# Order of two heads' products and Squares, of one subtraction, and the place of some weight tiles, in a hybrid decoder block

## The chip, the cores and the metric

The kernel runs on one core of one Trainium2 chip. The metric is the device time of one execution in microseconds (us), the median over several runs. A core has these engines: TensorE (PE in the profile; its weight loads, which overlap with its matmuls, are PEld), VectorE (DVE), ScalarE (ACT), GpSimd (POOL) and SyncE (SP), which here only issues transfers. Each engine has its own list of instructions and works through it in order; engines wait for each other on semaphores. SBUF is the on-chip memory that all engines read and write; PSUM is where TensorE puts its results, here cut into banks of 128 partitions x 512 fp32 numbers.

## The reference

One layer of a decoder block on x of 512 tokens by 1024 features, all in float32:

```
h   = rms_norm(x, norm_mix_pre)
proj = h @ w_in        # GLA q, k, v, r, a; NSA q and three branches' k, v; gates
A   = gla_mixer(...)   # chunked gated linear attention, 4 heads, dk 128, dv 256
B   = nsa_mixer(...)   # compressed, selected and window attention, 8 heads
mixed = sigmoid(merge_gla) * (A @ w_proj_gla) + sigmoid(merge_nsa) * (B @ w_proj_nsa)
x   = x + rms_norm(mixed @ w_out, norm_mix_post)
h   = rms_norm(x, norm_ffn_pre)
f   = (silu(h @ w_ffn_gate) * (h @ w_ffn_up)) @ w_ffn_down     # 1024 -> 2816 -> 1024
x   = x + rms_norm(f, norm_ffn_post)
```

The part of `gla_mixer` that the change touches, per head: the output of a chunk is the masked attention inside the chunk times v, plus q (with its decay) times the state before the chunk; then each token's 256 outputs are normalised by the root of their mean square and multiplied by a gate:

```
o = attn @ v + qe @ s_prev
o = o * rsqrt(mean(o * o) + eps) * norm_g
return o * silu(r)
```

## The kernel before, in words

**Three products for one.** A matrix in fp32 is split into a high part, rounded to the type fp32r, and a low part, the difference to it. `three` (L262 to L276) then makes one product out of three matmuls: high x high (L269), high weights x low data (L274), low weights x high data (L275). `prod` runs it over the 128-row blocks of the contraction. The product is [128 outputs, up to 512 tokens]; the activations h, transposed, lie in `hT` (`hT_hi`, `hT_lo`), the weights are the stationary operand. `split` (L299 to L303) makes the two parts: ScalarE writes the high one (L301), VectorE the low one (L303). For many weights `Stream.ahead_to` does the same at L103 and L110. A call of `restart()` makes the next product of 256 columns cut its second matmul into two of 128 columns.

**Fewer products.** Some large products are not done plainly but by a seven-product scheme for 2 x 2 blocks of matrices. Its units have seven products each, named `a11, s2, s3, s1, a22, s4, a12` after the weights' block or sum of blocks. In the first stage the units are those of the combined input projection (`EPAIRS`, functions `eproduct`, `eform`), in the last stage those of the down projection (`make`, `dsum`, `down_product`). Their matmuls have 256 columns, those of plain products 512.

**Weights in a ring.** `Ring` hands out the weight tiles: `whi0, wlo0, whi1, wlo1`, four tiles of 128 x 1024 fp32r that are used in turn. `Stream` loads a weight into a raw tile by a SyncE transfer, splits it into the next `whi` and `wlo`, and keeps one ahead of TensorE. Some keys have a place of their own (`place`) and take no ring tile. The ring is opened at the start (L181) and opened again at position 18 of the stream (`st.reset`, L119), at a new place of memory. Into the first ring go the weights of the token projection (keys `"tok"`), the forms of the seven-product units that `eplace` (L437) puts there two to a tile, and the plain products `with_gla`: GK0, GQ0, GK2, GQ2, MA0, MA1 (MA2 has a place of its own; MA3 lies in the second ring).

In the allocation of this kernel the first ring takes bytes 200,672 to 217,056 of a partition. Every tile in it starts at 224 modulo 256 bytes. `hT`, the moving operand of the plain products, starts at 160 modulo 256.

**The linear attention's stage**, about 60 to 227 us. `weave` lays the products of the seven-product units (main list) and the steps of the linear attention (side list) into one program order. `steps` has for head h: `gla_attn`, `gla_prep`, `gla_state`, `gla_out`, `gla_end`. `gla_out(h)` makes the head's output in four blocks n of 128 tokens, two blocks in each of two PSUM banks of the tag `acc`. For h of 0 and 1 a block is one or two plain fp32 matmuls (L806: attention x v; L808: q x state, from n = 1 on; each shows as two records in the trace), for h of 2 and 3 one or two calls of `three`. After each block ScalarE makes its Square with a sum over the 256 outputs (L809; it reads the bank and writes `go`):

```
out = ps[n // 2][:, (n % 2) * 256:(n % 2) * 256 + 256]
...
act.activation(out=o[:, n, :], in_=out, func=AF.Square, accum_out=ssq[:, n:n + 1])
```

The framework orders accesses by bank: an instruction that writes to a bank waits for an earlier one in program order that reads from it. Within the program order's dependences the framework may move instructions, so the trace has block 2 of head 1 ahead of block 1. Then follow the mean and root (`rsqrt_mean`, L317 on VectorE and L318 on GpSimd), the scaling of the four blocks (L817 on ScalarE), and in `gla_end` their transposes on TensorE (L832).

**The down projection's stage**, about 727 to 808 us. `seq` lists the seven-product units' products in order of use, number j; `make(j)` prepares the weights of product j some products ahead: `dsum` makes the sums and differences of raw blocks on VectorE, and `split` the two parts. Raw blocks are loaded on SyncE's queue as soon as a place is free (`dload`, L1899). The order on VectorE is the program order, except where `tc.issue_after(x)` puts an instruction behind x. The numbers that matter here: j = 7 is unit 1's `a11`, 8 `s2`, 9 `s3`, 10 `s1`, 11 `a22`, 12 `s4`, 13 `a12`. Unit 1's s4 is the block 12 of the raw weights less s2 (L1915), and the block 12 (`c_two`) is the last loaded. `lows[j]` is the low part's instruction of product j (L303).

Of the kernel before, what the change touches and what calls it, by code (L numbers as in the profile page):

```python
# [9 lines left out]
F32R = mybir.dt.float32r  # L10
U8 = mybir.dt.uint8
AF = mybir.ActivationFunctionType
OP = mybir.AluOpType
# [26 lines left out]
class Stream:  # L40
# [30 lines left out]
    def ahead_to(self, n, between=None):  # L71
        while self.made < min(n, self.limit or len(self.src)):
            i = self.made
            key, ap, cols = self.src[i]
            raw = self.raws.pop(i, None)
            if raw is None and key not in self.by_half:
                raw = self.fetch(i)
            if key in self.by_half:
                raw = self.pool.tile([128, 1024], F32, tag="wraw", bufs=3, name="wraw")
                hi = self.pool.tile([128, 1024], F32R, tag="whi", bufs=2, name="whi")  # L80
                lo = self.pool.tile([128, 1024], F32R, tag="wlo", bufs=2, name="wlo")
                big, small = ap
                b = big.shape[2]
                self.nc.scalar.dma_start(raw.rearrange("p (a t) -> p a t", a=2)[:, :, b:], small)
                for i2, c in enumerate((slice(0, cols // 2), slice(cols // 2, cols))):
                    self.nc.sync.dma_start(raw[:, c][:, :b], big[:, i2, :])
                    with self.tc.issue_after(last.ins) if i2 else nullcontext():
                        made = self.nc.vector.tensor_copy(hi[:, c], raw[:, c])
                    if i2 == 0:
                        last = between(made)  # L90
                    with self.tc.issue_after(last.ins):
                        self.nc.vector.tensor_tensor(out=lo[:, c], in0=raw[:, c], in1=hi[:, c].bitcast(F32),
                                                     op=OP.subtract)
                self.done[i] = (hi, lo)
                self.made += 1
                continue
            if key in self.place:
                hi, lo = self.place[key]()
            else:
                hi = self.pool.tile([128, 1024], F32R, tag="whi", bufs=2, name="whi")  # L100
                lo = self.pool.tile([128, 1024], F32R, tag="wlo", bufs=2, name="wlo")
            h, l, r = [self.part(key, x, cols) for x in (hi, lo, raw)]
            self.cast = self.nc.scalar.copy(h, r)  # L103
            if key in self.on_dma:

                self.nc.scalar.activation(out=l, in_=r, func=AF.Copy, scale=-1.0)  # L106
                self.nc.gpsimd.dma_start(l, r, accum_op=OP.add)  # L107
            else:
                with self.tc.issue_after(self.after.ins) if self.after else nullcontext():
                    self.nc.vector.tensor_tensor(out=l, in0=r, in1=h.bitcast(F32), op=OP.subtract)  # L110
                self.after = None
            self.done[i] = (hi, lo)
            self.made += 1
# [14 lines left out]
class Ring:  # L128
# [9 lines left out]
            self.pool[1].__exit__(None, None, None)  # L138
        self.pool = None

    def open(self, shift):

        self.close()
        p = self.tc.tile_pool(name="ring", bufs=1, reuse_waits="tile", side="right")
        self.pool = (p.__enter__(), p)
        self.turn = {"whi": 0, "wlo": 0}
        self.shift = shift

    def tile(self, shape, dtype, tag, bufs, name):
        if tag == "wraw":  # L150
            return self.raws.tile(shape, dtype, tag=tag, bufs=bufs, name=name)
        i = self.turn[tag]
        self.turn[tag] = i + 1
        t = self.pool[0].tile(shape, dtype, tag="%s%d" % (tag, i % 2), bufs=1, name=name)
        if self.shift and sum(self.turn.values()) == 4:
            self.pool[0].tile([128, self.shift], F32, name="shift")
        return t
# [17 lines left out]
def hybrid_block_kernel(ctx: ExitStack, tc: tile.TileContext, I, outT):  # L175
    nc = tc.nc
    act, dve, pool, pe = nc.scalar, nc.vector, nc.gpsimd, nc.tensor

    base = ctx.enter_context(tc.tile_pool(name="base", bufs=1, reuse_waits="tile"))
    wts = Ring(ctx, tc)  # L180
    wts.open(0)  # L181
    psum = ctx.enter_context(tc.tile_pool(name="psum", bufs=1, space=PSUM))

    def half_line(where):
# [55 lines left out]
    for key in with_gla + with_cmp + with_att + late:  # L240
        kind, n = key
# [343 lines left out]
    tok = [tokv.tile([128, 1024], F32, name="tok%d" % i) for i in range(NT)]  # L585
# [60 lines left out]
    lows = []  # L646
# [145 lines left out]
    def gla_out(h, after=None):  # L792
        q3, qk, ku, dec, kut, ss = gst[h]
        at = ats[h % 2]
        ps = [bank("acc"), bank("acc")]
        ssq = gt.tile([128, NT], F32, tag="gssq", bufs=2, name="gssq")
        o = gt.tile([128, NT, 256], F32, tag="go", bufs=1, name="go")
        for n in range(NT):
            out = ps[n // 2][:, (n % 2) * 256:(n % 2) * 256 + 256]
            if h >= 2:  # L800
                with tc.issue_after(after.ins) if after else nullcontext():
                    three(out, two_of[h, "a"][n], two_of[h, "v", n], True, n == 0)
                    if n > 0:
                        three(out, two_of[h, "q"][n], two_of[h, "s"][n - 1], False, True)
            else:
                pe.matmul(out, at[:, n, :], tok[n][:, h * 256:(h + 1) * 256], start=True, stop=(n == 0))  # L806
                if n > 0:
                    pe.matmul(out, q3[:, n].rearrange("p s t -> p (s t)"), ss[:, n - 1, :], start=False, stop=True)  # L808
            act.activation(out=o[:, n, :], in_=out, func=AF.Square, accum_out=ssq[:, n:n + 1])  # L809
        rs = gt.tile([128, NT], F32, tag="grs", bufs=2, name="grs")  # L810
        rsqrt_mean(rs, ssq, 256, EPS)

        def scaled(after=None):
            for n in range(NT):
                out = ps[n // 2][:, (n % 2) * 256:(n % 2) * 256 + 256]
                with tc.issue_after(after.ins) if after else nullcontext():
                    act.activation(out=o[:, n, :], in_=out, func=AF.Copy, scale=rs[:, n:n + 1])  # L817

        if h < 2:
            rest[h] = scaled  # L820
        else:
            scaled()
        gst[h] = o
# [1078 lines left out]
    def dsum(u, name, after=None):  # L1902
# [7 lines left out]
        elif name == "s1":  # L1910
            dve.tensor_tensor(out=r11, in0=r11, in1=draw[u, "s2"], op=OP.add)
            draw[u, "s1"] = r11
        elif name == "s4":
            x = draw[u, "s2"]
            dve.tensor_tensor(out=x, in0=r12, in1=x, op=OP.subtract)  # L1915
            draw[u, "s4"] = x


# [8 lines left out]
    def make(j):  # L1927
# [2 lines left out]
        u, a, b = seq[j]  # L1930
        behind = ends.get(j - 5) or ends.get(j - 7) if a == "s2" else None
        with tc.issue_after(behind.ins) if behind else nullcontext():
            dsum(u, a, (None, lows.get(7), None, ends.get(j - 3))[u])
        hi, lo = [x[:, :KW] for x in w_slot(("w", "g3", "w")[j % 3])]
        lows[j] = split(hi, lo, draw[u, a if a[0] == "s" else a[1:]])
        dw[u, a] = (hi, lo)
# [299 lines left out]
```

## Time and profile before

| | us |
|---|---|
| median of 3 runs | 829.97 (829.06 to 830.84) |
| profiled execution | 828.92 |
| its span | 826.7 |
| TensorE busy | 817.1 (99% of the span) |
| VectorE busy | 638.8 (77%) |
| ScalarE busy | 533.7 (65%) |
| GpSimd busy | 138.8 (17%) |

The profile is of one execution; the span goes from its first to its last recorded instruction, and 2.2 us of the execution's time lie outside it. A row of a timeline has the start in us from the span's start, the length in us, the engine, the line of the kernel, the operation, output and inputs by the program's names, the tile's shape, and the number of equal instructions that follow each other; in square brackets stands the idle time before it and what ended it. A matmul's length has its way through the array in it, and the next one starts before it ends: how long one takes in a stream is the distance from start to start. A row of a window has its limits, its length, the engine's busy time with the number of instructions, the granted clock of TensorE as a share of full speed, the busy share of the transfer engines and what they moved in GB/s.

### The profile page before, as it was taken

How to read it: one execution, taken by the hardware profiler on the slowest of the kernel's cores; microseconds unless marked ns; L12 is line 12 of the kernel's file. 1: busy time of each engine (PE TensorE's matmuls, PEld its weight loads, DVE VectorE, ACT ScalarE, POOL GpSimd, SP SyncE). 2: the span in 40 equal slices, each digit the busy share in tenths (PEclk: the TensorE clock that was granted, in tenths of full speed). 3: DMA queues.
4: the chain of work that ended last, by engine and by line, in shares of the span. 5: the costliest groups of instructions: out<-in, count | busy, mean ns of one | idle time of the engine just before them, and what ended most of it. 6: DMA issues, size and time to landing. Idle time of an engine off the chain costs nothing.

```text
span 826.7 us, 15082 instructions
## 1 busy us (share of the span) xinstructions
PE 817.1 (99%) x5751; PEld 751.2 (91%) x5751; DVE 638.8 (77%) x1216; ACT 533.7 (65%) x988; POOL 138.8 (17%) x172
## 2 busy tenths in 40 slices
PE   9999999999999999999999999999999999999997
PEld 7898899899888787888888999999999999999997
DVE  7776898886377888877666479998888778929886
ACT  6647677775544989887645577866665566626453
POOL 0101122230030000010000364111221110001134
PEclk9999999999999999999999999999999999999999
DMA  8434466764152444454227758798888883235233
GB/s 275 126 107 118 119 120 125 165 142 114 52 185 50 109 122 105 102 119 112 69 72 262 234 157 232 178 235 204 182 184 202 198 192 90 77 94 173 97 102 103
DMA packets 44824, 117.87 MB, mean 143 GB/s; under 512 B 5868, under 2 KB 12028, under 8 KB 44624
## 3 DMA queue, kind: packets, MB, share of 16 engines
q1 hardware_dynamic: 31584, 82.71, 32.5%
q0 software_dynamic: 12464, 33.85, 22.5%
q8 instruction: 45, 0.74, 0.4%
q10 hardware_dynamic: 704, 0.36, 0.1%
q14 instruction: 27, 0.22, 0.1%
HBM read 102.21 MB, written 4.19 MB: 129 GB/s over the span
## 4 chain that ended last, share of the span: by engine, by line
PE 89%; DVE 4%; ACT 4%; DMA 1%; issue 1%; POOL 0%; POOLq 0%; ACTq 0%; DVEq 0%
PE ps_mm L269 13%; PE ps_mm L274 13%; PE ps_mm L275 13%; PE ps_sc L269 5%; PE ps_sc L275 5%; PE ps_sc L274 4%; PE ps_acc L269 3%; PE ps_acc L274 3%; PE ps_acc L275 3%; PE ps_tp L275 3%; PE ps_tp L274 3%; PE ps_tp L269 3%; PE ps_sc L605 2%; PE ps_tp L605 2%; PE ps_tp L1246 2%; PE ps_mm L605 1%
## 5 line engine op out<-in xcount | busy, mean ns | idle before, releaser
L269 PE MATMUL ps_mm<-hT_hi,whi 128*128 128x512 f32 (+1 forms) x268 | 98.4, 367 | 0.0
L275 PE MATMUL ps_mm<-hT_hi,wlo 128*128 128x512 f32 (+1 forms) x268 | 96.9, 362 | 0.0
L274 PE MATMUL ps_mm<-hT_lo,whi 128*128 128x512 f32 (+1 forms) x267 | 96.3, 361 | 0.0
L103 ACT CAST whi<-wraw 128x1024 fp32r<-128x1024 f32 (+2 forms) x61 | 59.0, 970 | 51.2 <-PE ps_mm L274 15.3
L110 DVE TENSOR_TENSOR wlo<-wraw,whi 128x1024 fp32r<-128x1024 f32 (+2 forms) x46 | 50.1, 1091 | 29.9 <-ACT whi L103 29.8
L269 PEld LDWEIGHTS ps_mm<-hT_hi,whi 128*128 128x128 f32 x268 | 50.4, 188 | 8.1
L275 PEld LDWEIGHTS ps_mm<-hT_hi,wlo 128*128 128x128 f32 x268 | 50.4, 188 | 8.1 <-DVE wlo L110 0.3
L274 PEld LDWEIGHTS ps_mm<-hT_lo,whi 128*128 128x128 f32 x267 | 50.2, 188 | 6.6
L1576 ACT CAST d_two<-s 128x1024 fp32r<-128x1024 f32 x26 | 27.2, 1045 | 35.9 <-PE ps_mm L275 18.7
L303 DVE TENSOR_TENSOR pl<-ps_tp,ph 128x512 fp32r<-128x512 f32 (+1 forms) x64 | 31.2, 490 | 13.0 <-ACT ph L301 12.0
L1583 DVE TENSOR_TENSOR d_two<-s,d_two 128x1024 fp32r<-128x1024 f32 x25 | 30.6, 1225 | 11.3 <-ACT d_two L1576 10.9
L1208 ACT ACTIVATE p<-p,mx 128x512 f32<-128x512 f32 (+3 forms) x64 | 35.7, 558 | 4.6 <-DVE mx L1206 4.1
L1206 DVE CUSTOM_DVE_ANT_0 p<-ps_sc,causal 128x512 f32<-128x512 f32 (+3 forms) x64 | 30.1, 487 | 9.7 <-PE ps_sc L1200 8.9
L107 POOL DMA_DIRECT2D wlo<-wraw x15 | 12.7, 849 | 147.4 <-ACT wlo L106 90.2
L1981 POOL TENSOR_TENSOR y<-y,us 128x256 f32<-128x256 f32 x12 | 13.5, 1143 | 98.5 <-DVE us L1977 98.5
L301 ACT CAST ph<-ps_tp 128x512 fp32r<-128x512 f32 (+1 forms) x64 | 26.5, 416 | 4.4 <-PE ps_tp L1246 3.4
L1246 PE MATMUL ps_tp<-ident,p 128*128 128x128 f32 x160 | 27.7, 272 | 0.0
L1246 PEld LDWEIGHTS ps_tp<-ident,p 128*128 128x128 f32 x160 | 20.8, 141 | 7.2 <-ACT pc L1130 0.4
L1576 ACT CAST c_two<-s 128x1024 fp32r<-128x1024 f32 x12 | 12.5, 1044 | 20.3 <-PE ps_acc L275 10.5
L1558 POOL DMA_DIRECT2D wlo<-in_w_gate x13 | 11.2, 858 | 80.4 <-ACT wlo L1556 71.9
L269 PE MATMUL ps_mm<-hT_hi,d_two 128*128 128x256 f32 x80 | 22.4, 279 | 0.0
L275 PE MATMUL ps_mm<-hT_hi,d_two 128*128 128x256 f32 x80 | 22.3, 279 | 0.0
(905 smaller groups left out, 3299.5 us busy)
## 6 DMA issues: line engine op xcount, KB each, us to landing
wraw<-in_w_t SPq DMA_DIRECT2D x36, 512.0 KB, 4.0
wraw<-in_w_gate SPq DMA_DIRECT2D x21, 512.0 KB, 4.4
rw<-in_w_up SPq DMA_DIRECT2D x19, 512.0 KB, 8.2
wlo<-wraw POOLq DMA_DIRECT2D x15, 512.0 KB, 4.5
wlo<-in_w_gate POOLq DMA_DIRECT2D x13, 512.0 KB, 7.7
w_uu<-in_w_up POOLq DMA_DIRECT2D x19, 256.0 KB, 8.7
wraw<-in_w_proj SPq DMA_DIRECT2D x8, 512.0 KB, 3.5
wraw<-in_w_out SPq DMA_DIRECT2D x8, 512.0 KB, 4.3
```

What stands on the lines that cost most here:

```text
L103: self.cast = self.nc.scalar.copy(h, r)
L110: self.nc.vector.tensor_tensor(out=l, in0=r, in1=h.bitcast(F32), op=OP.subtract)
L269: pe.matmul(o, wh, xh, start=start, stop=False, skip_group_check=True)
L274: pe.matmul(o[:, c], wh, xl[:, c], start=False, stop=False, skip_group_check=True)
L275: stk["pe"] = pe.matmul(o, wl, xh, start=False, stop=stop, skip_group_check=True)
L303: return dve.tensor_tensor(out=lo, in0=src, in1=hi.bitcast(F32), op=OP.subtract)
L605: pe.matmul(o, x[:, k, t], y[:, w], start=(k == 0 and m == 0), stop=(k == KD - 1 and m == 2))
L1206: dve.tensor_tensor_reduce(out=o, in0=s, in1=causal[:, S - 128 * (i + 1):S], scale=-1.0, scalar=-NEG, op0=OP.add, op1=OP.min, accum_out=mx ...
L1208: act.activation(out=o, in_=o, func=AF.Exp, scale=-1.0, bias=mx[:, i:i + 1], accum_out=z[:, i:i + 1])
L1246: pe.transpose(tp[:, i * 128:(i + 1) * 128], p[:, OFF[i] + k * 128:OFF[i] + (k + 1) * 128] if i else p0, ident)
L1576: stk[names[0]] = act.copy(hi, t)
L1583: stk["lo"] = dve.tensor_tensor(out=lo, in0=t, in1=hi.bitcast(F32), op=OP.subtract)
```

## The change

Three edits that do not depend on each other.

1. In `gla_out` the Squares of blocks n - 1 and n are both issued in program order after the products of an odd n, where each had followed its own block's products.
2. In `dsum` the subtraction of unit 1's s4 is put behind `lows[j - 1]` on VectorE, the low part of product 11. The other units' s4 and the other sums stay as they were.
3. The first ring gets a little room: its `whi` tiles are 1072 wide and its `wlo` tiles 1040, and 1024 of that are used. A tile for a plain product (a key that is not `"tok"`) starts at element 48 of `whi` and at 0 of `wlo`; all others at 0 of `whi` and 16 of `wlo`. The ring's top stays, so that it begins 512 bytes lower, at byte 200,160 (224 modulo 256) of a partition. By these widths a plain tile comes to 160 modulo 256, and the others stay at 224. The second ring is opened without room, as before.

```diff
@@ Stream.ahead_to
-                hi = self.pool.tile([128, 1024], F32R, tag="whi", bufs=2, name="whi")
-                lo = self.pool.tile([128, 1024], F32R, tag="wlo", bufs=2, name="wlo")
+                plain = key[0] != "tok"
+                hi = self.pool.tile([128, 1024], F32R, tag="whi", bufs=2, name="whi", plain=plain)
+                lo = self.pool.tile([128, 1024], F32R, tag="wlo", bufs=2, name="wlo", plain=plain)
@@ Ring
-    def open(self, shift):
+    def open(self, shift, room=False):
         self.close()
+        self.room = room
...
-    def tile(self, shape, dtype, tag, bufs, name):
+    def tile(self, shape, dtype, tag, bufs, name, plain=False):
...
+        if self.room:
+            at = (0, 48) if tag == "whi" else (16, 0)
+            t = self.pool[0].tile([128, 1024 + max(at)], dtype, tag="%s%d" % (tag, i % 2), bufs=1, name=name)
+            return t[:, at[plain]:at[plain] + 1024]
@@ hybrid_block_kernel
-    wts.open(0)
+    wts.open(0, True)
@@ gla_out
-            act.activation(out=o[:, n, :], in_=out, func=AF.Square, accum_out=ssq[:, n:n + 1])
+            for m in range(n - 1, n + 1) if n % 2 else ():
+                act.activation(out=o[:, m, :], in_=ps[n // 2][:, (m % 2) * 256:(m % 2) * 256 + 256], func=AF.Square,
+                               accum_out=ssq[:, m:m + 1])
@@ dsum
         elif name == "s4":
             x = draw[u, "s2"]
-            dve.tensor_tensor(out=x, in0=r12, in1=x, op=OP.subtract)
+            with tc.issue_after(after.ins) if after and u == 1 else nullcontext():
+                dve.tensor_tensor(out=x, in0=r12, in1=x, op=OP.subtract)
@@ make
-            dsum(u, a, (None, lows.get(7), None, ends.get(j - 3))[u])
+            dsum(u, a, lows.get(j - 1) if a == "s4" else (None, lows.get(7), None, ends.get(j - 3))[u])
```

## The prediction, made before the result was known

> **What bounds the kernel now.** I read the page first.
>
> ```profile
> span 826.7 us, 15082 instructions
> PE 817.1 (99%) x5751; PEld 751.2 (91%) x5751; DVE 638.8 (77%) x1216; ACT 533.7 (65%) x988; POOL 138.8 (17%) x172
> ```
>
> TensorE is busy in 817.1 of 826.7 us; no other engine is above 77%. So an edit can win only where TensorE stands still, where it changes from one kind of matmul to another, or where one matmul takes longer than it need. The view of TensorE's waits, longest first, shows how little stands still:
>
> ```profile
> PE ps_acc L806 <- ACT go L809: 1.1, 1, 1.1
> PE ps_acc L215 <- DVE mhalf L200: 1.0, 1, 1.0
> ```
>
> So the third question matters most: how far apart do matmuls of one form start? The timeline of TensorE answers it for 512 columns, with first and last rows of two stretches of L269/L274/L275 alone (start, length, instruction):
>
> ```profile
> 89.75 0.40 PE L269 MATMUL ps_mm<-hT_hi,whi 128*128 128x512 f32 x1
> ...
> 97.92 0.39 PE L275 MATMUL ps_mm<-hT_hi,wlo 128*128 128x512 f32 x1
> ```
> ```profile
> 232.02 0.39 PE L269 MATMUL ps_mm<-hT_hi,whi 128*128 128x512 f32 x1
> ...
> 241.99 0.39 PE L275 MATMUL ps_mm<-gh,wlo 128*128 128x512 f32 x1
> ```
>
> 35 steps in 8.17 us are 233.4 ns each, 44 steps in 9.97 us are 226.6. For 256 columns I took windows with nothing else in them: length, busy time, matmuls (two of which were already running at the window's start), clock, DMA share, GB/s.
>
> ```profile
> 98.20:113.40 15.20, 15.20 (x131) 1.00 0.59 121
> 140.60:148.40 7.80, 7.80 (x71) 1.00 0.62 133
> 560.00:700.00 140.00, 140.00 (x1238) 1.00 0.78 181
> 771.00:808.00 37.00, 37.00 (x316) 1.00 0.31 101
> ```
>
> 15.20/129 = 117.8 ns, 7.80/69 = 113.0, 140.00/1236 = 113.3, 37.00/314 = 117.8. The clock is 1.00 in all and the slow stretches move the fewer bytes, so neither explains it. A 256-column stream has two paces and keeps one over a thousand matmuls.
>
> **The change, part by part.** The profiled execution took 828.92 us: the span of 826.7 and 2.2 outside it. It lies 1.05 below the median of 829.97. I sum against 828.92 and add 1.05 at the end.
>
> *Products ahead of Squares (`gla_out`).* No instruction is added or removed. Two n share a PSUM bank, so the product of n = 1 waited for the Square of n = 0 and that of n = 3 for the Square of n = 2. Head 1, TensorE and then ScalarE and VectorE:
>
> ```profile
> 160.76 1.02 PE L806 MATMUL ps_acc<-tok,at 128*128 128x256 f32 x4
> 161.62 0.59 PE L808 MATMUL ps_acc<-gs,gq 128*128 128x256 f32 x2
> 163.35 0.70 PE L806 MATMUL ps_acc<-tok,at 128*128 128x256 f32 x2 [1.14 <-ACT go L809]
> 163.89 0.59 PE L808 MATMUL ps_acc<-gs,gq 128*128 128x256 f32 x2
> ```
> ```profile
> 161.79 0.62 ACT L452 CAST whi<-wraw 128x512 fp32r<-128x512 f32 x1 [2.00 <-PE ps_acc L806]
> ...
> 162.84 0.36 ACT L809 ACTIVATE go<-ps_acc 128x256 f32<-128x256 f32 x1
> ```
> ```profile
> 161.80 0.69 DVE L388 TENSOR_TENSOR wraw<-wraw 128x512 f32<-128x512 f32 x1 [0.42 <-DMA wraw<-in_w_t]
> ```
>
> Four records of L806 take 161.62 - 160.76 = 0.86, so 0.215 each. The products of n = 0 and 2 run, then n = 1 waits for the first Square at 162.84, which is queued on ScalarE behind a cast whose data landed late (VectorE's row says so). The pair at 161.62 should end its issue at 162.05 and the next starts at 163.35: 1.30 lost; the two records after it take 0.54 for 0.43: 0.11. Head 1 is worth 1.41.
>
> Head 0 came in three visits; the last:
>
> ```profile
> 134.17 0.28 PE L269 MATMUL ps_mm<-et2gh,whi 128*128 128x256 f32 x1
> 134.52 0.70 PE L806 MATMUL ps_acc<-tok,at 128*128 128x256 f32 x2
> 135.06 0.59 PE L808 MATMUL ps_acc<-gs,gq 128*128 128x256 f32 x2
> ```
>
> 0.35 instead of 0.12 to enter and 0.54 instead of 0.43 behind it: 0.34. I take 0.3 for head 0; ends 0 (a wait for something else stands there) and 0.34. Heads 2 and 3 use three-part products. Their rows where a product follows a Square, first in head 2, then in head 3, and each head's transposes:
>
> ```profile
> 199.31 0.28 PE L274 MATMUL ps_acc<-gsgl,gqe 128*128 128x256 f32 x1
> 199.57 0.39 PE L269 MATMUL ps_acc<-tok,gah 128*128 128x256 f32 x1
> 199.79 0.28 PE L274 MATMUL ps_acc<-tok,gah 128*128 128x256 f32 x1
> ...
> 206.80 1.03 PE L832 MATMUL ps_tp<-ident,go 128*128 128x128 f32 x8
> ...
> 219.31 0.28 PE L274 MATMUL ps_acc<-gsgl,gqe 128*128 128x256 f32 x1
> 219.57 0.38 PE L269 MATMUL ps_acc<-tok,gah 128*128 128x256 f32 x1
> 219.80 0.28 PE L274 MATMUL ps_acc<-tok,gah 128*128 128x256 f32 x1
> ...
> 225.48 1.25 PE L832 MATMUL ps_tp<-ident,go 128*128 128x128 f32 x8
> ```
>
> 0.26 and 0.22 where 0.12 is the pace: 0.24 in each head. Head 3's transposes last 0.22 longer than head 2's, because the scaled blocks come late; products without a break bring the last Square forward, which should pay that. Head 2: 0.24, head 3: 0.45. Sum of this part: 1.41 + 0.3 + 0.24 + 0.45 = 2.4; ends 1.0 (head 1 alone, less 0.4 for a wait further on) and 2.44. What the edit delays is the Square of n = 0; behind it stand only the other Squares and the scaling, which needs all four anyway. No DMA is moved.
>
> *The sum behind a low part (`dsum`).* VectorE, TensorE and the chain of waits in the down stage:
>
> ```profile
> 766.81 1.09 DVE L1915 TENSOR_TENSOR c_two<-c_two 128x896 f32<-128x896 f32 x1 [1.01 <-DMA c_two<-in_w_down]
> 767.82 1.09 DVE L303 TENSOR_TENSOR wlo<-wraw,whi 128x896 fp32r<-128x896 f32 x1
> ...
> 770.15 1.08 DVE L303 TENSOR_TENSOR wlo<-wraw,whi 128x896 fp32r<-128x896 f32 x1
> ```
> ```profile
> 768.62 0.28 PE L274 MATMUL ps_tp<-dt3hl,whi 128*128 128x256 f32 x1
> 768.96 0.39 PE L275 MATMUL ps_tp<-dt3e,wlo 128*128 128x256 f32 x1
> 769.18 0.28 PE L269 MATMUL ps_tp<-dt3e,whi 128*128 128x256 f32 x1
> ...
> 776.25 0.28 PE L269 MATMUL ps_tp<-hT_hi,whi 128*128 128x256 f32 x1
> ```
> ```profile
> 760.82 5.89 DMA c_two<-in_w_down
> ```
>
> The subtraction of s4 waits on VectorE until its transfer has landed, 1.01 us idle, and the low part queued behind it (767.82) is the one that L275 needs at 768.96. That step is 0.34 for 0.113, the next 0.22: 0.33 lost. After the change this low part runs in the idle 1.01, and the subtraction stands behind the low part of 770.15, from about 771.3 to 772.4. Next late is its own cast (about 0.95 on ScalarE) and its low part (1.1): ready at 774.4. Its product starts at 776.25 and with what is won here before it (0.33, and 65 matmuls x 4.5 ns = 0.3) at 775.6: 1.2 us of cover, so I cost the move at nothing; without the cover it would cost what is late, up to 1.
>
> The stop at 768.62 is also where the pace goes from 113.3 to 117.8. If the stream is not interrupted, I expect it to keep 113.3: 314 matmuls of the last window, with those up to 771, about 335, x 4.5 ns = 1.5 us. Ends: 0 and 1.5. I take 1.5, as the 140 us of the third window kept it. Part: 1.85.
>
> *Weights 64 bytes lower (`Ring`).* In the kernel's allocation hT lies at 160 and every ring tile at 224, modulo 256 bytes of a partition. The wider tiles put the plain ones at 160. The stretch at 89.75 has weights 64 bytes off the moving operand, that at 232.02 has 0. Only GK and GQ twice and MA0, MA1 use this ring as plain tiles: 6 products x 24 = 144 matmuls x 6.8 ns = 0.98. Ends: 0 (place is not the cause) and 0.98; I take 0.7, nearer the upper end, as the first matmuls of each product may not be at their pace yet. The pair that follows at 98.2 inherits its pace from this stream: 129 x 4.5 = 0.6 if it falls to 113.3; even odds, so 0.3. The other entries into 256-column streams are drawn again, +-0.7. No instruction is added; the ring's larger reach only holds memory that nothing else uses at that time.
>
> The Trainium skill speaks against this part: "SBUF — State Buffer", Who interferes with whom, gives TensorE two independent read ports, one for the moving operand and one for weights, and lets TensorE wait on nobody. By that rule the places of two operands can't matter and this part is worth 0; the rows at 89.75 and 232.02 show two paces that the rule does not have.
>
> Sum: 2.4 + 1.85 + 0.7 + 0.3 = 5.25, less 0.5 because TensorE, coming earlier, meets transfers that did not move (161.80 is one). 4.75.
>
> **Rivals.**
>
> 1. *The pace does not hold in the down stage.* For: a pace is drawn at each interruption, and there are other ones near 768. Against: the third window. It costs 1.5: 826.7.
>
> 2. *Head 1's wait comes back.* The forms made at 161.79 are late because their data lands then; TensorE now arrives 1.4 earlier and waits for them in a later product. For: the row with 0.42 of waiting for that transfer. Against: no TensorE wait for such a form is among the longest. It costs 1.4: 826.6. With the first, 828.1.
>
> 3. *Place doesn't matter.* The last part gives neither 0.7 nor 0.3: 826.2. For: the two stretches above differ in more than the place. Against: nothing else in them differs by row or clock.
>
> 4. *Slower: a flip in the feed-forward stretch.* It holds 113.3 from one split matmul to the next:
>
> ```profile
> 555.01 0.33 PE L274 MATMUL ps_mm<-hT_lo,d_two 128*128 128x128 f32 x2
> ...
> 708.98 0.33 PE L274 MATMUL ps_sc<-hT_lo,whi 128*128 128x128 f32 x2
> ```
>
> One short stop of TensorE behind 555, because a ScalarE or transfer order has shifted, would leave the rest at 117.8: (708.98 - 555.01)/0.1133 = 1359 matmuls x 4.5 = 6.1 us: 831.3. It decides, that is eats the whole gain of 4.75, if it comes before 589 (4.75/4.5 ns = 1056 matmuls, 119.6 us before 708.98). For: 768.62 did just that. Against: nothing in the edits touches that stretch.
>
> **How the numbers follow.** 828.92 - 4.75 = 824.2 on the profiled basis, 825.2 on the median's. Chances: forecast 0.48, rival 1 0.16, rival 2 0.10, rival 3 0.08, two of these together or entries drawn badly (828 to 830) 0.09, rival 4 0.09. The range for 8 in 10 goes from 823.3 (1.9 less: 0.3 more from the places, 0.3 from the pair at 98.2, 0.5 without the loss to transfers, and 0.7 and a little for the entries) to 828.4 (rivals 1 and 2 together). About 0.2%, 1.66 us, is what a measurement of this kernel can tell from no change: faster means under 828.3, slower above 831.6. The first four cases are faster but for a remainder: 0.78. The fifth and half of the fourth rival: 0.14 the same. Half of rival 4 and mishaps with it: 0.08 slower.
>
> **What would show it.** Right: no wait of L806 for L809 around 161; L809 rows in twos behind n = 1 and n = 3; L303 at about 765.8 ahead of L1915; no step over 0.12 near 768.6 and over 325 matmuls in a window of the same 37 us there; 512-column steps of 227 before 98 and at 194 to 210. Wrong: a new wait of TensorE for a form between 165 and 180, a last window at 117.8, steps still at 233, or a count under 1230 in the 140 us behind 560.

## The result, and the profile after

The changed kernel takes 824.7 us (median of 6 runs, 823.91 to 826.72), the kernel before in the same comparison 829.43 (6 runs, 827.67 to 830.84). The ratio is 0.9947 with a 95% interval of 0.9930 to 0.9963: 4.4 us less, between 3.1 and 5.8 (the two medians themselves lie 4.7 apart). The forecast was 825.2 in a range of 823.3 to 828.4. The profiled execution has a span of 822.2 where the one before had 826.7.

In what follows line numbers of the changed kernel are higher than before: L813 and L815 are the plain products of `gla_out` (L806, L808), L276, L281 and L282 the three matmuls (L269, L274, L275), L310 the low part (L303), L1925 the subtraction of s4 (L1915), L841 the transposes (L832).

The page of the changed kernel, and the first and last of the four rows in its view of TensorE's waits:

```profile
span 822.2 us, 15085 instructions
PE 813.2 (99%) x5751; PEld 748.8 (91%) x5751; DVE 638.2 (78%) x1216; ACT 534.3 (65%) x988; POOL 138.5 (17%) x172
```
```profile
PE ps_acc L222 <- DVE mhalf L207: 1.1, 1, 1.1
...
PE ps_mm L612 <- DVE whi L88: 0.6, 1, 0.6
```

The wait of a product for a Square, first of the list before, is gone. The second row of the four is a wait of 0.7 for GpSimd at 28.8 us, far ahead of the change; the first profile of the kernel before does not have it, its second profile has it with 0.5. TensorE is as bound as it was, and busy for 4 us less. Its timeline at head 1, head 2, head 3's transposes, the second product at 92 us, product 9 of the down projection and that stage's end:

```profile
92.59 0.39 PE L282 MATMUL ps_mm<-hT_hi,wlo 128*128 128x512 f32 x1
...
98.03 0.39 PE L282 MATMUL ps_mm<-hT_hi,wlo 128*128 128x512 f32 x1
...
160.44 1.02 PE L813 MATMUL ps_acc<-tok,at 128*128 128x256 f32 x4
161.30 0.59 PE L815 MATMUL ps_acc<-gs,gq 128*128 128x256 f32 x2
161.74 0.59 PE L813 MATMUL ps_acc<-tok,at 128*128 128x256 f32 x2
162.17 0.59 PE L815 MATMUL ps_acc<-gs,gq 128*128 128x256 f32 x2
...
197.01 0.28 PE L276 MATMUL ps_acc<-tok,gah 128*128 128x256 f32 x1
197.13 0.28 PE L281 MATMUL ps_acc<-tok,gah 128*128 128x256 f32 x1
...
222.54 1.04 PE L841 MATMUL ps_tp<-ident,go 128*128 128x128 f32 x8
...
765.60 0.28 PE L281 MATMUL ps_tp<-dt3hl,whi 128*128 128x256 f32 x1
765.71 0.28 PE L282 MATMUL ps_tp<-dt3e,wlo 128*128 128x256 f32 x1
...
803.45 0.28 PE L282 MATMUL ps_sc<-hT_lo,wlo 128*128 128x256 f32 x1
803.83 0.61 PE L317 MATMUL ps_tp<-ones,acc 128*128 128x1 f32 x4
```

The plain products of head 1 follow each other without a break. The two steps of head 2 that were 0.26 and 0.22 are down to the pace, as the one from 197.01 to 197.13 shows, head 3's eight transposes last 1.04 and not 1.25, and there is no stop at product 9. From 92.59 to 98.03 are 24 steps, 226.7 ns each. The last two rows are new: 0.38 where 0.11 is the pace, a wait for the sums at the end of the stage.

VectorE in the down stage, and TensorE's window there, with the earlier line's columns:

```profile
764.22 1.09 DVE L310 TENSOR_TENSOR w_g3l<-wraw,w_g3h 128x896 fp32r<-128x896 f32 x1 [0.60 <-ACT w_g3h L308]
...
766.60 1.35 DVE L310 TENSOR_TENSOR wlo<-wraw,whi 128x896 fp32r<-128x896 f32 x1 [0.42 <-ACT whi L308]
767.87 1.08 DVE L1925 TENSOR_TENSOR c_two<-c_two 128x896 f32<-128x896 f32 x1
...
770.03 1.09 DVE L310 TENSOR_TENSOR wlo<-c_two,whi 128x896 fp32r<-128x896 f32 x1 [0.76 <-ACT whi L308]
```
```profile
767.00:803.00 36.00, 36.00 (x321) 1.00 0.30 96
```

The subtraction now comes behind product 11's low part, and no longer waits for its transfer. Product 12's low part is done at 771.1 and needed at 772.9, so the move costs nothing. 36.00/319 = 112.9 ns: the faster pace.

Where both traces pass the same matmul, and what each stretch contributed (starts in us, from the span's start):

| until | before | after | change in the stretch |
|---|---|---|---|
| first token sum in the attention stage | 65.22 | 65.73 | +0.51 (nothing of the change lies here; the wait at 28.8 us) |
| a product just ahead of head 0 | 127.42 | 127.54 | -0.39 (places 0.40, less a new stop of 0.24; the rest paces) |
| a product between heads 0 and 1 | 156.38 | 156.06 | -0.44 |
| product behind head 1 | 168.02 | 166.20 | -1.50 |
| MA0 | 194.29 | 192.55 | +0.08 |
| head 3's last transpose | 226.45 | 223.30 | -1.41 (heads 2 and 3 -1.2, places the rest) |
| product 9 of the down projection | 768.51 | 765.49 | +0.13 |
| product 12 | 776.25 | 772.62 | -0.61 |
| TensorE's last instruction | 820.92 | 816.45 | -0.84 |

The row of -0.39 can't be put down to the places as a whole: the same stretch took 61.64 to 62.21 in nine profiles of kernels that lack one edit or more, 61.77 in two that have none, as its 256-column streams ran at one pace or the other. What belongs to the places is read from their own products below.

### The profile page after: what moved, and what is told of

It reads as the page before. It is cut to its first block, busy times and chain, and to the rows that moved or that the text cites. A ratio compares the mean times of both kernels' runs of the same rounds, so it can differ in the third digit from the quotient of the medians.

```text
span 822.2 us, 15085 instructions
## 1 busy us (share of the span) xinstructions
PE 813.2 (99%) x5751; PEld 748.8 (91%) x5751; DVE 638.2 (78%) x1216; ACT 534.3 (65%) x988; POOL 138.5 (17%) x172
## 4 chain that ended last, share of the span: by engine, by line
PE 90%; DVE 3%; ACT 3%; issue 1%; DMA 1%; POOL 1%; SPq 0%; POOLq 0%; ACTq 0%; DVEq 0%
PE ps_mm L276 14%; PE ps_mm L281 14%; PE ps_mm L282 14%; PE ps_sc L276 4%; PE ps_sc L282 4%; PE ps_sc L281 4%; PE ps_acc L276 4%; PE ps_acc L282 4%; PE ps_acc L281 4%; PE ps_tp L282 3%; PE ps_tp L276 3%; PE ps_tp L281 3%; PE ps_tp L612 2%; PE ps_tp L1255 2%; PE ps_sc L612 1%; PE ps_acc L612 1%
## 5 line engine op out<-in xcount | busy, mean ns | idle before, releaser
L276 PE MATMUL ps_mm<-hT_hi,whi 128*128 128x512 f32 (+1 forms) x268 | 98.1, 366 | 0.0
L282 PE MATMUL ps_mm<-hT_hi,wlo 128*128 128x512 f32 (+1 forms) x268 | 96.6, 360 | 0.0
L281 PE MATMUL ps_mm<-hT_lo,whi 128*128 128x512 f32 (+1 forms) x267 | 96.0, 360 | 0.0
L276 PEld LDWEIGHTS ps_mm<-hT_hi,whi 128*128 128x128 f32 x268 | 50.4, 188 | 7.9
L282 PEld LDWEIGHTS ps_mm<-hT_hi,wlo 128*128 128x128 f32 x268 | 50.3, 188 | 7.9 <-DVE wlo L111 0.3
L281 PEld LDWEIGHTS ps_mm<-hT_lo,whi 128*128 128x128 f32 x267 | 50.2, 188 | 6.5
L310 DVE TENSOR_TENSOR pl<-ps_tp,ph 128x512 fp32r<-128x512 f32 (+1 forms) x64 | 31.2, 490 | 13.0 <-ACT ph L308 12.1
L108 POOL DMA_DIRECT2D wlo<-wraw x15 | 12.7, 849 | 147.4 <-ACT wlo L107 80.9
L276 PE MATMUL ps_mm<-hT_hi,d_two 128*128 128x256 f32 x80 | 22.3, 279 | 0.0
L282 PE MATMUL ps_mm<-hT_hi,d_two 128*128 128x256 f32 x80 | 22.3, 278 | 0.0
```

What stands on the lines that cost most here:

```text
L276: pe.matmul(o, wh, xh, start=start, stop=False, skip_group_check=True)
L281: pe.matmul(o[:, c], wh, xl[:, c], start=False, stop=False, skip_group_check=True)
L282: stk["pe"] = pe.matmul(o, wl, xh, start=False, stop=stop, skip_group_check=True)
L310: return dve.tensor_tensor(out=lo, in0=src, in1=hi.bitcast(F32), op=OP.subtract)
```

## The experiments

### One edit at a time

Three kernels, each the kernel before with one of the three edits as in the diff above.

> The kernel before with the order of products and Squares alone. My theory (a product of the second block of a bank waits for the Square of the first): the wait of head 1 is gone and stays gone, 2.4 us less than the kernel before, within 1.6 to 2.8; the stretch between the products of heads 0 and 3 carries it and nothing changes from 230 us on. Rival (the wait comes back where TensorE meets a form that was late anyway): at most 1.0 less, and a new row in the view of TensorE's waits.

Measured: 825.34 us beside 828.78 (12 and 35 runs), ratio 0.9964 (0.9952 to 0.9977): 3.0 us less, between 1.9 and 4.0, where 1.6 to 2.8 was expected. In the trace head 0's stretch falls from 9.00 to 8.58, head 2's from 9.72 to 9.25, head 3's from 9.35 to 8.67, head 1's from 8.78 to 7.28; no wait of a product for a Square and no new one behind. The mechanism is as expected; the size lies a little above the range. But this kernel, which has the old order in the down stage, showed neither the stop nor the slow pace there:

```profile
766.30 0.28 PE L274 MATMUL ps_tp<-dt3hl,whi 128*128 128x256 f32 x1
766.42 0.28 PE L275 MATMUL ps_tp<-dt3e,wlo 128*128 128x256 f32 x1
```
```profile
766.00:801.00 35.00, 35.00 (x312) 1.00 0.36 114
```

Product 9's third matmul starts 0.12 behind the second, and 35.00/310 = 112.9 ns.

> The kernel before with the subtraction of unit 1's s4 behind the low part alone. My theory: 0.33 us from the stop at 768.62 and 1.5 from the pace of 113.3 ns, which holds to the end of the stage: 1.85 less, within 1.4 to 2.0. Rival (the pace of this stretch comes from elsewhere): 0.33 less, and the windows behind 771 stay at 117.8 ns.

Measured: 827.84 beside 828.78, ratio 0.9996 (0.9984 to 1.0008): between 1.3 less and 0.7 more. That is not the 1.85 of the theory, and no clear gain at all. In its trace the stop is gone and the stage runs at 113.3 ns; but so did the kernel above without this edit.

> The kernel before with the places of the plain tiles alone. My theory (weights and moving operand at the same place modulo 256 bytes let a 512-column matmul start after 226.7 ns and not 233.4): 0.7 us less, within 0.2 to 1.3 with the 256-column stream behind it. Rival (the place does not matter): within 0.3 of the kernel before, and the two kinds of pace of 512-column streams mixed at random. The profile of the whole change speaks for something between: the first product still steps by 233, the others by 227.

Measured: 828.18 beside 828.78, ratio 0.9993 (0.9980 to 1.0006), which takes in both theories. The trace separates them: the 23 steps of the second product at 92 us are 226.7 ns each (233.4 before, 233.3 in the kernel with the sum alone). The two products up to 98 us take 0.31 less (10.96 for 11.27), GK0 and GQ0 with what lies between 0.20, the two stretches at 194 to 210 us 0.12 and 0.11: 0.74 in all. Something is given back: behind the first product of the pair at 98 us TensorE now waits, by the profile for a copy of ScalarE, and two steps there are 0.27 and 0.22 long, some 0.25 lost. The first twelve steps of the pair take 1.56 for 1.41; in the five profiles with these places and no added cuts they take 1.52 to 1.57, in the eight without these places 1.36 to 1.41. In its down stage TensorE stopped longer than before and kept the fast pace all the same:

```profile
767.39 0.28 PE L281 MATMUL ps_tp<-dt3hl,whi 128*128 128x256 f32 x1
768.08 0.38 PE L282 MATMUL ps_tp<-dt3e,wlo 128*128 128x256 f32 x1 [0.41 <-DVE wlo L310]
```
```profile
770.00:803.00 33.00, 33.00 (x294) 1.00 0.36 115
```

A stop of 0.58 (0.69 less the step), then 33.00/292 = 113.0 ns. A stop is not enough to set the slow pace.

### Is the place the cause, and the pace a state?

```diff
@@ Ring.tile, the kernel with the places alone
-            at = (0, 48) if tag == "whi" else (16, 0)
+            at = (0, 16) if tag == "whi" else (48, 0)
```

> As the kernel with the places alone, but with the plain tiles at 32 modulo 256 bytes, 128 bytes away from the moving operand (element 16 of whi and 0 of wlo; the others at 0 and 48). My theory (only the same place modulo 256 brings 226.7 ns): the two products at 87 to 98 us step by 230 or more, and nothing is gained beside the kernel before. Rival (any place but 64 bytes away, or chance): steps of 227 there and 0.3 to 0.7 less.

Measured: 828.26 beside 828.30, ratio 0.9997 (0.9980 to 1.0014). The 23 steps at 92 us are 232.1 ns each, and the two products up to 98 us take 11.22 (11.27 before, 10.96 with the places of the change). So room in the ring does nothing; of the three distances tried, 64, 128 and 0, only 0 is fast. The time alone could not have told it. The moving operand stayed where it was in all of these kernels, so they do not separate the distance from the weights' place itself. This run also has a small hitch at 754.77, far ahead of product 9, and behind it the slow pace:

```profile
754.77 0.32 PE L276 MATMUL ps_mm<-hT_hi,w_g3h 128*128 128x256 f32 x1
754.92 0.28 PE L281 MATMUL ps_mm<-hT_hi,w_g3h 128*128 128x256 f32 x1
```
```profile
757.50:803.00 45.50, 45.50 (x389) 1.00 0.40 135
709.00:754.00 45.00, 45.00 (x400) 1.00 0.29 80
```

A step of 0.15 for 0.11 was enough: 45.50/387 = 117.6 ns behind it, 45.00/398 = 113.1 ahead.

```diff
@@ hybrid_block_kernel, the kernel before
     for j, (u, a, b) in enumerate(seq):
+        if j == 10:
+            restart()
         end = down_product(j)
```

> The kernel before with no edit of the change, but with the second matmul of product 10 of the down projection cut in two of 128 columns, as at the other restarts. It leaves the stop at 768.62 in place. My theory (a pace is a state, set at an interruption and kept until the next; a cut matmul sets the faster one): the stop still costs 0.33, the windows from 772 on are at 113.3 ns, and the time is 1.4 us less. Rival (the 117.8 comes from what the other engines and transfers do there, or from the late sums): nothing gained, the windows stay at 117.8.

Measured: 828.4 beside 828.78, ratio 1.0000 (0.9987 to 1.0014): no gain of 1.4. The trace shows the mechanism as expected, though:

```profile
768.61 0.39 PE L275 MATMUL ps_tp<-dt3e,wlo 128*128 128x256 f32 x1
768.84 0.28 PE L269 MATMUL ps_tp<-dt3e,whi 128*128 128x256 f32 x1
...
770.95 0.28 PE L269 MATMUL ps_tp<-dt1e,w_g3h 128*128 128x256 f32 x1
771.07 0.33 PE L274 MATMUL ps_tp<-d_two,w_g3h 128*128 128x128 f32 x2
```
```profile
772.00:803.00 31.00, 31.00 (x276) 1.00 0.33 108
```

Behind the stop 18 steps take 2.11 us, 117 ns each; behind the cut matmul 31.00/274 = 113.1. So the pace is a state that an interruption can change either way, and a cut can set it back. That it was worth nothing in the median fits with the other profiles of kernels without the edit of the sum, of which only two in seven are in the slow pace there.

```diff
@@ the changed kernel
     def eproduct(u, i):
+        restart()
...
     def ffn_half(e, w, ps, ks=range(KD)):
+        restart()
...
     def out_half(n, e):
+        restart()
```

> The changed kernel, with the second matmul cut in two at the start of every product of the first seven-product units and of every call of the half-width products between 455 and 520 us. Theory (each interruption draws the pace again, a cut matmul sets the faster one and costs nothing): the 256-column steps at 117.8 between 80 and 200 us and between 470 and 520 us fall to 113.3, by the steps in the changed kernel's trace 2.2 us in all; 1.2 to 2.4 less than the changed kernel. Rival (the cut matmul costs something each time, or the pace is set by the weights' and data's places): no gain on the changed kernel, or slower.

Measured: 837.38 beside 828.30 for the kernel before, ratio 1.0105 (1.0085 to 1.0126): 8.7 us slower than before and some 12.7 slower than the changed kernel. A cut is not free, as I had assumed:

```profile
107.03 0.28 PE L276 MATMUL ps_mm<-hT_hi,feq 128*128 128x256 f32 x1
107.15 0.33 PE L281 MATMUL ps_mm<-hT_lo,feq 128*128 128x128 f32 x2
...
107.49 0.28 PE L276 MATMUL ps_mm<-hT_hi,feq 128*128 128x256 f32 x1
```

Three matmuls take 0.46 where three uncut ones take 0.34. The page counts 5,843 matmuls for 5,751, so 92 more: 92 x 0.113 = 10.4 us, most of the loss. Some of the rest are waits of 0.2 to 0.6 us that the changed kernel does not have. Nor does a cut always set the faster pace: behind 9 of the 63 cuts between 77 and 201 us the steps stayed at 117.5 ns or more. Where it does, it pays by these numbers from some 25 matmuls of the slow pace on (0.113/0.0045).

### How much is drawn anew in each execution?

> The kernel before once more, unchanged, for its profile alone: which of its stops are drawn anew in each execution? If head 1's wait hangs on when a transfer lands, the stretch of 159 to 168 us lies anywhere from 7.3 to 8.8 us; if the 117.8 ns of the down stage is a drawn state, it may be 113.3 this time. If both are fixed in the kernel, they come back as 8.78 us and 117.8 ns.

Measured: one run of 826.88 us, span 824.7, and a profile without any of the stops on which much of my sum rested. Head 1 of this second profile of the kernel before, and its down stage:

```profile
161.36 1.02 PE L806 MATMUL ps_acc<-tok,at 128*128 128x256 f32 x4
162.22 0.59 PE L808 MATMUL ps_acc<-gs,gq 128*128 128x256 f32 x2
162.66 0.59 PE L806 MATMUL ps_acc<-tok,at 128*128 128x256 f32 x2
```
```profile
160.83 0.62 ACT L452 CAST whi<-wraw 128x512 fp32r<-128x512 f32 x1 [0.40 <-DMA wraw<-in_w_t]
...
161.99 0.39 ACT L809 ACTIVATE go<-ps_acc 128x256 f32<-128x256 f32 x1
```
```profile
770.00:803.00 33.00, 33.00 (x294) 1.00 0.33 104
```

ScalarE's cast, held by the transfer, began 0.53 ahead of the first product; in the first profile it began 1.03 behind it (161.79 and 160.76). The Square then comes in time, and n = 1 follows without a wait. The transfer behind that cast took 4.64 us from issue to landing here and 6.27 in the first profile. Count the cast's start from the product 1.5 us ahead of the head, in all kernels without added copies: with the old order, starts of 0.79 to 1.12 go with stretches of 7.26 to 7.35, and starts of 1.92 to 2.61 with 8.05 to 8.78. With the new order a start of 1.83 still goes with 7.28. The down stage runs at 33.00/292 = 113.0 ns.

> The changed kernel once more, for its profile alone. Theory: 7.28 us in head 1's stretch again, because nothing is left to wait for; 0.43 less in head 0 (8.57 between its two marks), 0.45 to 0.7 less in heads 2 and 3; the down stage at 113.3 ns unless something else stops TensorE there.

Measured: 824.78 us, span 822.6; head 1's stretch 7.35, head 0's 8.56, head 2's and 3's as in the changed kernel, down stage at the fast pace. As expected.

### Making ScalarE late on purpose

```diff
@@ gla_out, in both kernels, ahead of the loop over n
+        for _ in range(3 if h == 1 else 0):
+            act.copy(o[:, 2:4, :].rearrange("p a b -> p (a b)"), at.rearrange("p n t -> p (n t)"))
```

> The kernel before with three extra copies of 128x512 on ScalarE (some 0.52 us each by the rows of its casts) ahead of the first Square of head 1, which writes over what they leave. Theory (before the change, TensorE's second block of a bank waits for the first block's Square, so that all lateness of ScalarE in head 1 reaches TensorE): a wait of L806 for L809 of 1 to 2.7 us in head 1, in whatever state the transfer lands, and 0.8 to 1.6 more than the kernel before. Rival (the wait of 1.14 in the first profile was a matter of the late transfer alone, and ScalarE has slack for the copies): no wait above 0.6, same time.

> The changed kernel with the same three copies at the same place. Theory (after the change no product of head 1 waits for a Square): no wait of a product in head 1, the stretch from 159 to 168 us as in the changed kernel (7.28 us between the products named et3gh and hT there) to 0.3, and at most 0.3 more than the changed kernel in time. Rival (lateness only moves to the forms behind the Squares on ScalarE): a new wait of TensorE of 0.5 us or more between 163 and 180 us.

Measured: the kernel before with the copies 828.11 beside 829.14 (ratio 0.9989, 0.9970 to 1.0008), the changed one with them 825.36 (0.9956, 0.9937 to 0.9976). The copies did not do what they were for: ScalarE took them at 150 to 155 us, in idle time. The profile of the first is of use for another reason, since in it the transfer landed latest of all, 7.05 us behind its issue:

```profile
163.30 0.62 ACT L452 CAST whi<-wraw 128x512 fp32r<-128x512 f32 x1 [2.81 <-DMA wraw<-in_w_t]
...
164.35 0.36 ACT L811 ACTIVATE go<-ps_acc 128x256 f32<-128x256 f32 x1
```
```profile
161.41 1.02 PE L808 MATMUL ps_acc<-tok,at 128*128 128x256 f32 x4
162.27 0.59 PE L810 MATMUL ps_acc<-gs,gq 128*128 128x256 f32 x2
164.86 0.82 PE L808 MATMUL ps_acc<-tok,at 128*128 128x256 f32 x2 [2.00 <-ACT go L811]
165.47 1.06 PE L810 MATMUL ps_acc<-gs,gq 128*128 128x256 f32 x2
```

The cast is 1.51 later than in the first profile (163.30 and 161.79), and so is the product that resumes (164.86 and 163.35). Head 1's stretch is 11.19. In the changed kernel with the copies it is 7.34, with a transfer of 4.90.

```diff
@@ gla_out, the kernel before (the changed kernel: (h, n) == (1, 1))
+            for _ in range(5 if (h, n) == (1, 0) else 0):
+                act.copy(o[:, 3, :], out)
             act.activation(out=o[:, n, :], in_=out, func=AF.Square, accum_out=ssq[:, n:n + 1])
```

> The kernel before with five copies of 128x256 on ScalarE out of the bank of head 1's first product, ahead of its Square; since they read that product they cannot run early, as the three copies of the late kernels did (ScalarE took them in idle time at 150 to 155 us). By the step from one Square to the next half of a bank (0.26 to 0.28 us) they hold ScalarE 1.3 to 1.4 us. Theory (a bank's second product waits for all that reads its first): TensorE waits in head 1 in every execution, the stretch between the marks et3gh and hT is 8.4 us or more (7.3 without a wait), and the time at least 0.8 more than the kernel before. Rival (slack on ScalarE takes it): stretch under 8, same time.

> The changed kernel with the same five copies, out of head 1's first bank, behind its two products and ahead of their Squares. Theory: no product of head 1 waits; the stretch between the marks stays at 7.3 us and the time within 0.4 of the changed kernel. Rival (ScalarE, 1.3 us later, holds up a form that TensorE needs next): a stop of 0.3 us or more between 163 and 180 us and 0.5 to 1.3 more.

Measured: 828.87 beside 829.79 (ratio 0.9993, 0.9981 to 1.0006) and 825.7 (0.9948, 0.9929 to 0.9966). The theory for the first failed: its stretch is 7.63, not 8.4, and the time is not longer. The framework had put the held products elsewhere:

```profile
162.39 0.48 PE L269 MATMUL ps_mm<-et1gh,whi 128*128 128x256 f32 x1
...
163.52 0.70 PE L806 MATMUL ps_acc<-tok,at 128*128 128x256 f32 x2
...
165.07 0.59 PE L806 MATMUL ps_acc<-tok,at 128*128 128x256 f32 x2
```

Lateness that is written into the program was filled here with matmuls of another product; the waits that these profiles show came with a transfer, whose lateness the program does not hold. In the second kernel the copies did hold the Squares: counted from the same product ahead of the head, the first began after 4.86 us, where it was 2.99 in the second profile of the changed kernel. Head 1's stretch was 7.35 all the same, as expected, and no stop above 0.2 followed up to 180 us. So with the new order Squares that are 1.9 us late cost nothing here. Its profile is also the only one of a kernel with all three edits that fell into the slow pace: from 758 to 804 us 391 matmuls, 117.6 ns each, behind steps of 0.23 at 750.50 and 0.16 at 755.27. So the edit of the sum does not guard the pace.

## Why the prediction was right, point by point

The number was right, 825.2 for 824.7, and so was the sign of each edit's cause in the attention stage. But two terms stood for events of one execution, and one of them did not belong to the edit.

*Head 1, 1.41.* The mechanism is right, the size is that of one draw. Six profiles of kernels with the old order and no copies in this stage gave 8.78, 8.74, 8.05, 7.35, 7.28 and 7.26 for the stretch, by when the transfer landed; five with the new order gave 7.28 to 7.35. On the mean over these the edit is worth 0.6 here, and 1.1 with the profile of 11.19, whose copies ran in idle time and whose transfer was merely the latest. It takes a risk away rather than a cost.

*Heads 0, 2 and 3, 0.3 + 0.24 + 0.45.* Undersized: 0.43, 0.47 and 0.68, and these came back in every profile. In head 0 two visits to the plain products replace three, and none waits. In heads 2 and 3 the step and the one behind it are gone from both places where a product had followed a Square, of which I priced one. With head 1's 0.6 to 1.1 this part is 2.2 to 2.7, for 2.4 forecast; the time of this edit alone says 1.9 to 4.0.

*Squares' lateness at nothing.* Held: no form behind them became late, and the rival with a new wait (2) did not happen in any profile.

*The sum, 1.85.* Here a step failed: "If the stream is not interrupted, I expect it to keep 113.3." It does; but I took the slow pace of one profile for what the kernel does. Of seven profiles of kernels without this edit, and without a cut there, two had the slow pace (the first profile, and the places at 128, from 754 us on), and of five with it one had it. The stop itself, with the slower step behind it, was worth anything from 0 to 0.72; it is what the edit seems to take away, since none of the five kernels with it stopped at product 9 and four of the seven without it did, one by 0.03 only. The pace is worth less than its steps, too: from product 12 to the end the first profile took 44.67 and that of the changed kernel 43.83, 0.84 less where some 270 steps of 4.5 ns make 1.2, in part because the faster one then waits for sums at 803.45. The edit alone measured 0.3, with an interval that holds zero; rival 1, with 1.5 less to gain, describes it better than the forecast.

*Places, 0.7.* Right, and for the reason given, as far as these runs separate it: some 0.6 between the two profiles' products in question, 0.74 with this edit alone. In five profiles with a distance of 0 the second product at 92 us steps by 226.7 ns, in the seven at 64 bytes by 233.2 to 233.4. The Trainium skill, "SBUF — State Buffer", Who interferes with whom, would have this part at nothing; the steps of 226.7, 232.1 and 233.4 ns at distances of 0, 128 and 64 bytes speak against it. Rival 3 falls on the trace; on the time alone it could not be refuted.

*The pair at 98.2, 0.3.* Not there: 14.20 where it was 14.13. A fast stream ahead of it did not pass its pace on: the first steps are 117.7 as before. Then comes the stop for ScalarE's copy, 0.24 long in all, and behind it 70 steps at 113.6 win back about what it cost. The forecast had a pace that is inherited; these steps show one that changed at a stop.

*Less 0.5, for transfers that did not move.* What TensorE meets by coming earlier is that stop of 0.24, for a copy and not a transfer. The +0.08 and +0.13 in the table are no more than the same stretches differ by between kernels without any edit there.

*Rival 4, the flip in the feed-forward stretch.* In 13 profiles, all but that of the kernel with more cuts, the stretch from the cut at 555 us to that at 709 took 153.95 to 153.98 us. It did not happen once.

Why the total came out nonetheless: in part by luck, as 2.15 of the 5.25 forecast, the part of `dsum` and that of the pair, were mostly not there. One by one the edits measured 3.0, 0.3 and 0.6, 3.9 together, within the 3.1 to 5.8 of the whole change. What came back in every profile is 1.6 from heads 0, 2 and 3 and 0.6 from the places, less some 0.2 for the stop: 2.0 together. The second profiles of the two kernels, in which neither head 1 nor the down stage stops, have spans of 824.7 and 822.6, 2.1 apart.

The rest of the measured 4.4 has to come from what the kernel before meets in some executions and the changed one does not, its stops above all. The profiled execution before held about 2.5 of it (2.0 longer in span than the second profile, with about 0.5 less around 28 us), and so does a usual run: the medians of 828.3 to 829.8 lie 1.4 to 2.9 above the 826.88 of the second profiled execution, while the changed kernel's median of 824.7 lies at the 824.78 of its second one. So the profile I summed from was bad in its stops but typical in their sum. Head 1 accounts for 0.6 to 1.1 of that rest on the mean, the stop and the pace of the down stage for some tenths: with the 2.0 that makes some 3.0 to 3.5, at the lower end of the measured interval. Where what then remains lies, if anything does, stays open, as one or two profiles per kernel are too few to say.

## What to carry to other kernels

A stop in a profile may be there in one execution and not in the next: before it goes into a sum, profile a second execution, and price it by how often it is there. An order in which the bound engine needs nothing from a lagging one is worth having even where the profile shows no wait, since it takes away what a late transfer can do. A few parts in a thousand are found in the trace, by steps and by stretches between the same two instructions, where the time of an edit alone cannot tell them from nothing.

## What the runs showed of the hardware

*Operands' places.* In these kernels a 512-column fp32r matmul starts after 226.7 ns where weights and moving operand lie at the same place modulo 256 bytes, and after 232.1 or 233.4 at 128 or 64 bytes apart, at the same granted clock of 1.00. It takes a while to get there: at 64 to 67 us of the changed kernel's profile, behind transposes, matmuls with a distance of 0 still stepped by 229 to 236, and by 226 or 227 only from 68.2 us until the next interruption.

*A pace is kept.* The 256-column streams here run at 113.3 or 117.8 ns, the same instructions of the same kernel at one in one profile and at the other in the next. They keep a pace for hundreds of matmuls and can change it at interruptions down to 0.04 us. A stop of 0.58 left it as it was.

*After a stop of 2.2 us the clock was lower.* In the profile with the latest transfer TensorE stood from about 162.7 to 164.9. Its steps in plain fp32 behind it were 0.43, twice the usual 0.215, and the granted clock was 0.50 from 165.4 to 168.6. Two windows behind the stop, and a third later:

```profile
164.90:167.60 2.70, 2.70 (x7) 0.58 0.49 79
167.60:169.00 1.40, 1.40 (x8) 0.60 0.22 38
169.00:171.00 2.00, 2.00 (x20) 1.00 0.00 0
```

Of the 3.9 us that head 1 lost there, 2.2 are the stop and 1.6 the clock. The stop of 1.3 us in the first profile did not have it: the clock stayed at 1.00. One profile shows it, so where between the two lengths it begins, and on what else it hangs, stays open.
